# The MLP's second product with seven quarter products in place of eight

## The chip, the cores and the metric

The kernel runs on one core of a Trainium2 chip. The metric is the time of one execution on the device, in microseconds (us). TensorE (PE) multiplies matrices, VectorE (DVE), ScalarE (ACT) and GpSimd (POOL) work on elements, SyncE (SP) issues most of the loads and stores.

## The reference

One decoder block for 512 tokens of 1024 features in float32: a mixer (latent attention and a convolution branch, gated), then an MLP, each behind a norm and with a residual:

```python
m = hybrid_mixer(rms_norm(x, norm_mix_pre), ...)
x = x + rms_norm(m, norm_mix_post)
f = jnp.square(jax.nn.relu(rms_norm(x, norm_mlp_pre) @ w_ff1)) @ w_ff2   # 1024 -> 4096 -> 1024
x = x + rms_norm(f, norm_mlp_post)
```

Only the MLP's second product, `@ w_ff2`, and the steps behind it are touched.

## The kernel before

Every float32 operand of a product is split in two parts of 32 bits that PE takes in one pass each (type fp32r): ACT casts the high part, DVE (or POOL) subtracts it from the original for the low part. A product is then three matmuls (`mm3`, lines 84 to 88): high by high, high by low, low by high. A matmul takes a stationary tile of 128 x 128 and a moving tile of 128 x 512 and adds into one PSUM bank of 128 x 512. There are eight banks, under four tags: `ps` (three), `sc` (two), `cv` (two), `tp` (one).

Weights come through `wsplit` (line 99): SP loads 256 KB pieces into `raw` (six buffers), ACT casts (line 111) into `whi`, DVE subtracts (line 112) into `wlo` (four buffers each).

The first product of the MLP computes 32 tiles of 128 hidden features by 512 tokens. Tile j is eight `mm3` over the input features (`ff1_part`, line 685), into a bank `pf`; `ff1_end` (line 694) takes relu on ACT (line 696) and multiplies relu by the bank on DVE (line 699), which is the squared relu. The results stay in SBUF as 16 tiles `f1[p]` of two hidden blocks each. The first four tiles (`BRIDGE`) start on the first 256 tokens, while the last tokens' norms still run.

The second product (lines 730 to 741) holds its whole output, 4 token tiles by 2 halves of 512 columns, in the eight banks `po`. For each of the 32 hidden blocks it loads and splits one row block of w_ff2 (two pieces), splits the block of `f1` (`ff2_lhs`, line 713), and adds eight `mm3` to the banks. The last two blocks (`TAIL`) are done token tile by token tile (lines 751 to 757), so that the post-norm of one tile runs beside the products of the next: sums of squares on ACT (line 647), the inverse root on POOL (lines 649 and 145), multiplication by the gain on DVE (line 762), scale and residual on DVE (line 747), and stores by SP (line 748).

The order on each engine's queue is made when the kernel is built, by a planner: it goes through the program in written order of priority, but places an instruction when its data and a buffer are there by its own reckoning of time. A buffer of a tag is handed on when the last reader of the tile in it is done. On the chip each queue then runs in that fixed order.

The rotating buffers that matter here: `s` (six of 128 x 512, `stile`), `h` (four of 128 x 2048, of `hpool`, which hold the merged branches before), `sw` (four of 128 x 2048, which hold the MLP's input h2 in two parts), `w` (fourteen of 128 x 1024) and `ra` (four of 128 x 1024).

Of the kernel before, what the change touches and what calls it, by code (L numbers as in the profile page):

```python
# [58 lines left out]
def decoder_block(ctx: ExitStack, tc: tile.TileContext, a: dict, out: bass.AP):  # L59
# [15 lines left out]
    def stile(name, dt=F32):  # L75
        return spool.tile([P, 512], dt, tag="s", name=name, bufs=6)
# [7 lines left out]
    def mm3(o, lh, ll, rh, rl, first, last):  # L84
        """o += (lh + ll)^T (rh + rl) without the product of the two low parts (below float32's last bit)"""
        pe.matmul(o, lhsT=lh, rhs=rh, start=first, stop=False)  # L86
        pe.matmul(o, lhsT=lh, rhs=rl, start=False, stop=False)  # L87
        return pe.matmul(o, lhsT=ll, rhs=rh, start=False, stop=last)  # L88
# [10 lines left out]
    def wsplit(src, name, sizes=(512, 512), dst=None, eng=None):  # L99
        """load columns of src in pieces, split each; returns the piece (hi, lo) that holds a column range"""  # L100
        parts, off = [], 0
        for p, n in enumerate(sizes):
            raw = rtile(f"{name}_{p}", n)
            sp.dma_start(raw, src[:, off:off + n])
            if dst is None:
                hi = stage.tile([P, 512], F32R, tag="whi", name=f"whi_{name}_{p}", bufs=NSPLIT)[:, :n]
                lo = stage.tile([P, 512], F32R, tag="wlo", name=f"wlo_{name}_{p}", bufs=NSPLIT)[:, :n]
            else:
                hi, lo = (d[:, off:off + n] for d in dst)
            e = eng or pool  # L110
            recent[act] = act.copy(hi, raw)  # L111
            recent[e] = e.tensor_tensor(lo, raw, f32(hi), ALU.subtract)  # L112
            parts.append((off, n, hi, lo))
            off += n

        def cols(c0, n):
            for o, m, hi, lo in parts:
                if o <= c0 and c0 + n <= o + m:
                    return hi[:, c0 - o:c0 - o + n], lo[:, c0 - o:c0 - o + n]
            raise ValueError(f"columns {c0}:{c0 + n} of {name} lie in two pieces")  # L120

        return cols
# [53 lines left out]
    def rotary():  # L176
        """rotary tables: rows repeat every 32 partitions, sin carries the sign of its half"""
        ang = stile("ang")
# [15 lines left out]

    # the tensor engine's clock rises while it works: products that nothing reads, until the first data are there
    warm = tps("warm")
    for i in range(NWARM):
        pe.matmul(warm[:, :P], lhsT=ones, rhs=ones, start=i == 0, stop=i == NWARM - 1)

    # ---- first columns of W_in (latents, shared rope key), token rows; the pre-norm's scale of a token is  # L200
    # applied to its row of the product ----
    sp.dma_start(vecs, a["vecs"])
    xT = []
    with ExitStack() as s1:
        r1 = open_pool(s1, "r1")
        w0 = []
        for k in range(KD):
# [6 lines left out]
            w0.append(wsplit(a["w_z0"][k], f"z0{k}", (QL, Z0 - QL), (hi, lo), pool if k % 2 else dve))  # L214
        # squares of the stream, behind the splits that the first products wait for
        with ExitStack() as behind:
# [28 lines left out]
        def latents(t):  # L245
            """norms of the latents of token tile t; shared rope key, twice"""
            pa, pb = zt[t]
# [16 lines left out]
        def latents_t(t, c):  # L264
            """normalised latents to feature rows"""
            sl = slice(t * P, (t + 1) * P)
            for src, j0, n, x in ((c[0], 0, 3, "a"), (c[1], 3, 2, "b")):
                pp = cvtile(f"ct{x}{t}")
                for j in range(3):
                    pe.transpose(pp[:, j * P:(j + 1) * P], src[:, j * P:(j + 1) * P], ident)  # L270
                split_psum(cT[0][:, j0:j0 + n, sl], cT[1][:, j0:j0 + n, sl],
                           pp[:, :n * P].rearrange("p (j t) -> p j t", j=n))
            act.copy(krT[:, sl], pp[:, KL:KL + P])

        def token_scales():
            """rstd of the tokens, by partition and along the rows"""
            st_x = tps("st_x")
# [44 lines left out]

# [1 line left out]
    us = []  # L324
# [46 lines left out]
    def rope(z, name):  # L371
        """rotary embedding of two stacked heads (rows of 64), fp32"""
        sw = stile(f"sw_{name}")
# [26 lines left out]

# [1 line left out]
    att, vts, sts, qks, pms, pTs = [], {}, {}, {}, {}, {}  # L402
    with ExitStack() as s3:
        r2 = open_pool(s3, "r2")

        def project_pair(pr):
            """values (token rows) and rotary queries of a pair of heads"""
            w = wsplit(a["w_pair"][pr], f"pair{pr}", (512, QL))
# [14 lines left out]
            qr = rope(pq, f"q{pr}")  # L423
            # hi and lo of one head stacked over the rows
            st = [r2.tile([P, S], F32R, tag="qs", name=f"qs{pr}{j}", bufs=4) for j in range(2)]
# [6 lines left out]
        def project(h):  # L432
            """scaled queries and keys of a head without the rotary part, feature rows, split"""
            w = wsplit(a["w_head"][h], f"head{h}", (QL, KL))
# [78 lines left out]

# [1 line left out]
    r3 = open_pool(ctx, "r3")  # L515
# [29 lines left out]

    # causal depthwise convolution; running channel sum for the layer norm
    cs = []
# [27 lines left out]

    # layer norm over channels (partitions); sums over them through the tensor engine
    mub = cvtile("mub")
# [35 lines left out]

    # pointwise projection, gated merge
    wo = []
# [19 lines left out]

    # output projection, post-norm, residual, MLP pre-norm
    while len(wo) < KD:
# [5 lines left out]
    def square_sums(src, name, jk=None):  # L643
        """rsqrt of the mean square of two halves, plus eps"""
        ss = stat(f"ss_{name}", 2)
# [56 lines left out]
    for t in range(NT):  # L702
        prev = project_out(t, (lambda: norms(t - 1, prev)) if t else (lambda: None))
# [1 line left out]
    early = []  # L705
# [6 lines left out]

    def ff2_lhs(j):
        fh, fl = stile(f"fh{j}", F32R), stile(f"fl{j}", F32R)
        split_psum(fh, fl, f1[j // 2][:, j % 2, :])
        return fh, fl

    for j in range(NF):
        if j == NF - 2:
            first = ff2_lhs(0)  # L720
        if j < BRIDGE:
            pf, w = early[j]
            ff1_part(pf, w, SPLIT, S)
        else:
            w = wsplit(a["w_ff1"][j], f"f1{j}", eng=dve)
            pf = ps(f"pf{j}")
            ff1_part(pf, w, 0, S)
        ff1_end(j, pf)
    gout = gain("g_out", a["norm_mlp_post"], D)
    order = [tps] + [scs] * 2 + [cvtile] * 2 + [ps] * 3  # L730
    po = [[order[2 * t + hf](f"po{t}{hf}") for hf in range(2)] for t in range(NT)]
    ops = []
    for j in range(NF):
        w = wsplit(a["w_ff2"][j], f"f2{j}", eng=dve)
        fh, fl = ff2_lhs(j) if j else first
        ops.append((w, fh, fl))
        if j < NF - TAIL:
            for t in range(NT):
                sl = slice(t * P, (t + 1) * P)
                for hf in range(2):  # L740
                    mm3(po[t][hf], fh[:, sl], fl[:, sl], *w(hf * 512, 512), j == 0, False)

    def finish(t, o_, r):
        for c, n in ((0, 512), (512, 512)) if t < NT - 1 else ((0, 512), (512, 256), (768, 256)):
            hf, c1 = divmod(c, 512)
            piece = o_[:, hf, c1:c1 + n]
            dve.scalar_tensor_tensor(piece, piece, r, x1[t][hf][:, c1:c1 + n], ALU.mult, ALU.add)  # L747
            sp.dma_start(out[t * P:(t + 1) * P, c:c + n], piece)

    prev = None  # L750
    for t in range(NT):
        sl = slice(t * P, (t + 1) * P)
        o_ = wtile(f"o{t}")
        for hf in range(2):
            for j in range(NF - TAIL, NF):
                w, fh, fl = ops[j]
                mm3(po[t][hf], fh[:, sl], fl[:, sl], *w(hf * 512, 512), False, j == NF - 1)
            if hf == 0 and prev:
                finish(*prev)
        r = square_sums(po[t], f"o{t}", wtile(f"jo{t}"))  # L760
        for hf in range(2):
            dve.tensor_tensor(o_[:, hf, :], po[t][hf], gout[:, hf * 512:(hf + 1) * 512], ALU.mult)
        prev = t, o_, r
    finish(*prev)


def _layout(i):
    """Inputs as the kernel's loads take them: only reordered."""
    def rows(w):  # [K, N] -> [N/128, 128 (row in block), K/128 * 128 columns of one block]
        k, n = w.shape  # L770
        return w.reshape(k // P, P, n // P, P).transpose(2, 1, 0, 3).reshape(n // P, P, -1)
# [54 lines left out]
```

## Time and profile before

| | |
|---|---|
| time of three runs | 842.12 us median (841.9 to 844.08) |
| span of the profiled execution | 842.8 us |
| busy in that span | PE 824.0, DVE 518.8, ACT 377.0, POOL 210.1 us |
| matmuls of the second product | 768 |
| HBM read over the span | 76.76 MB |

The profile is one execution; the page gives its time as the span and lists nothing around it, so the span is its own time, and it lies inside the three runs' spread. The stretches of interest are the end of the mixer with the first tiles of the MLP (473 to 503 us), the first product (503 to 657), the second product (657 to 836), and the tail behind the last matmul (836 to 842.8). Busy times count an instruction from its start to its end, and on PE and DVE the listed times of neighbours overlap.

### The profile page before, as it was taken

Reading aid. Unit: us, or ns where it says so; the run is one execution under the profiler, and the core shown is the slowest. Engines: PE = TensorE matmul, PEld = TensorE weight load, DVE = VectorE, ACT = ScalarE, POOL = GpSimd, SP = SyncE. Lnnn points to the kernel's source line nnn. Section 1 sums busy time; section 2 is a strip of 40 time slices with the busy share of each in tenths; the row PEclk is TensorE's granted clock in tenths of the full one; section 3 lists DMA queues with packets and bytes.
Section 4 is the critical chain, followed back from the end, with each engine's and each line's share of the span. In section 5 each row is a group of like instructions: output and inputs, shape, how many; then the busy total and the mean of one; then the engine's idle time right before and its main releaser. Section 6 shows DMA issues by size and latency. Waiting matters only on the chain. (4 is left out here: it accounts for less than half of the span.)

```text
span 842.8 us, 10881 instructions
## 1 busy us (share of the span) xinstructions
PE 824.0 (98%) x3882; PEld 683.4 (81%) x3882; DVE 518.8 (62%) x838; ACT 377.0 (45%) x724; POOL 210.1 (25%) x201
## 2 busy tenths in 40 slices
PE   8989999999999999899999999999999999999996
PEld 8977888887878887687778898888888888888885
DVE  5689999999999986595554533333333333333335
ACT  7567775767572224365343333332333323332333
POOL 4244433434445446548611100000000000000001
PEclk9999999999999999899999999999999999999999
DMA  8412121222113324246440113232323232223312
GB/s 258 137 40 89 51 79 51 64 66 81 63 63 101 94 95 128 69 149 204 162 151 1 51 51 101 88 100 89 99 94 94 88 100 91 88 98 100 96 54 100
DMA packets 45126, 79.57 MB, mean 94 GB/s; under 512 B 5264, under 2 KB 10256, under 8 KB 45072
## 3 DMA queue, kind: packets, MB, share of 16 engines
q1 hardware_dynamic: 44640, 77.30, 29.0%
q0 software_dynamic: 432, 1.57, 0.5%
q8 instruction: 30, 0.49, 0.2%
q14 instruction: 24, 0.20, 0.1%
HBM read 76.76 MB, written 2.10 MB: 94 GB/s over the span
## 5 line engine op out<-in xcount | busy, mean ns | idle before, releaser
L112 DVE TENSOR_TENSOR wlo_f<-raw_f,whi_f 128x512 fp32r<-128x512 f32 x124 | 85.5, 690 | 213.3 <-ACT whi_f L111 213.1
L111 ACT CAST whi_f<-raw_f 128x512 fp32r<-128x512 f32 x124 | 76.6, 619 | 227.7 <-PE po L88 116.5
L559 DVE SCALAR_TENSOR_TENSOR cv<-u,convw,cv 128x512 f32<-128x512 f32 x232 | 161.8, 746 | 0.2
L87 PE MATMUL po<-wlo_f,fh 128*128 128x512 f32 x256 | 101.1, 395 | 0.0
L86 PE MATMUL po<-whi_f,fh 128*128 128x512 f32 x256 | 101.0, 395 | 0.0
L88 PE MATMUL po<-whi_f,fl 128*128 128x512 f32 x256 | 101.0, 395 | 0.0
L88 PE MATMUL pf<-h2h,wlo_f 128*128 128x512 f32 (+1 forms) x256 | 97.4, 381 | 0.0
L87 PE MATMUL pf<-h2l,whi_f 128*128 128x512 f32 (+1 forms) x256 | 97.4, 381 | 0.0
L86 PE MATMUL pf<-h2h,whi_f 128*128 128x512 f32 (+1 forms) x256 | 97.4, 380 | 0.0
L649 POOL TENSOR_SCALAR v_o<-ss_o 128x1 f32<-128x1 f32 x4 | 1.2, 302 | 351.5 <-ACT jo L647 351.5
L87 PEld LDWEIGHTS po<-wlo_f,fh 128*128 128x128 f32 x256 | 48.2, 188 | 11.4 <-DVE wlo_f L112 0.2
L88 PEld LDWEIGHTS po<-whi_f,fl 128*128 128x128 f32 x256 | 48.2, 188 | 11.3
L86 PEld LDWEIGHTS po<-whi_f,fh 128*128 128x128 f32 x256 | 48.2, 188 | 11.2
L112 POOL TENSOR_TENSOR wlo_gt<-raw_gt,whi_gt 128x512 fp32r<-128x512 f32 x32 | 43.9, 1374 | 50.5 <-ACT whi_gt L111 50.5
L88 PEld LDWEIGHTS pf<-h2h,wlo_f 128*128 128x128 f32 x256 | 48.2, 188 | 9.9
L87 PEld LDWEIGHTS pf<-h2l,whi_f 128*128 128x128 f32 x256 | 48.2, 188 | 9.9
L86 PEld LDWEIGHTS pf<-h2h,whi_f 128*128 128x128 f32 x256 | 48.3, 188 | 9.8
L86 PE MATMUL pg<-hTh,whi_gt 128*128 128x512 f32 x128 | 51.8, 405 | 0.0
L88 PE MATMUL pg<-hTh,wlo_gt 128*128 128x512 f32 x128 | 50.6, 395 | 0.0
L87 PE MATMUL pg<-hTl,whi_gt 128*128 128x512 f32 x128 | 50.6, 395 | 0.0
L111 ACT CAST whi_gt<-raw_gt 128x512 fp32r<-128x512 f32 x32 | 19.8, 618 | 41.3 <-PE pg L87 38.2
L86 PEld LDWEIGHTS pg<-hTh,whi_gt 128*128 128x128 f32 x128 | 24.6, 192 | 5.6 <-issue 0.5
(274 smaller groups left out, 1884.1 us busy)
## 6 DMA issues: line engine op xcount, KB each, us to landing
raw_f<-in_w_ff SPq DMA_DIRECT2D x128, 256.0 KB, 2.8
raw_gt<-in_w_zm SPq DMA_DIRECT2D x32, 256.0 KB, 2.6
raw_gb<-in_w_zm SPq DMA_DIRECT2D x16, 256.0 KB, 2.7
raw_ga<-in_w_zm SPq DMA_DIRECT2D x16, 256.0 KB, 2.6
raw_wo<-in_w_o SPq DMA_DIRECT2D x16, 256.0 KB, 2.7
raw_pw<-in_w_pw SPq DMA_DIRECT2D x16, 256.0 KB, 2.9
raw_wout<-in_w_out SPq DMA_DIRECT2D x16, 256.0 KB, 3.0
xT<-in_x_t SPq DMA_DIRECT2D x8, 256.0 KB, 4.2
```

Of the source, the lines that this page charges most:

```text
L86: pe.matmul(o, lhsT=lh, rhs=rh, start=first, stop=False)
L87: pe.matmul(o, lhsT=lh, rhs=rl, start=False, stop=False)
L88: return pe.matmul(o, lhsT=ll, rhs=rh, start=False, stop=last)
L111: recent[act] = act.copy(hi, raw)
L112: recent[e] = e.tensor_tensor(lo, raw, f32(hi), ALU.subtract)
L559: dve.scalar_tensor_tensor(co[j] if tap == CW - 1 else acc[j], src, convw[:, i, tap:tap + 1], acc[j], ALU.mult, ALU.add)
L649: pool.tensor_scalar(v, ss[:, 0:1], ss[:, 1:2], EPS, ALU.add, ALU.add)
```

## The change

The output is cut in quarters: two halves of the tokens by two halves of the columns. So are the hidden activations of a pair of blocks (two blocks by two halves of the tokens) and the four quarters of w_ff2 that belong to them (two blocks by two halves of the columns). A Strassen 2x2 scheme makes the four output quarters from seven products of quarters, for which sums and differences of quarters are formed first. Each of the seven has two banks (two token tiles of 128), and sums over the 16 pairs.

Three of the seven are computed in the loop over the first product's tiles: after each pair of tiles `first_operands` loads the pair's four quarters, forms three differences or sums of them and two of the activations, and splits them; `first_sweep` then adds the pair before to six banks (18 matmuls). While that lasts the first product's tiles have two banks left, of tag `ps`.

The other four follow behind it: `second_operands` loads the four quarters of w_ff2 again, forms one difference, splits the quarters and the activations, and `second_products` adds 24 matmuls for a pair. The three first results are copied and combined into `e`, `g` and `h` in SBUF (they free their banks). The last two pairs are done token tile by token tile, and the output quarters are put together by DVE additions (one in each token tile on POOL) before the post-norm, which now reads them from SBUF. Lines up to 712 stand as before, but for comments. The new part, cut to its core:

```diff
-    for j in range(NF):
-        ...
-    po = [[order[2 * t + hf](f"po{t}{hf}") for hf in range(2)] for t in range(NT)]
-    for j in range(NF):
-        w = wsplit(a["w_ff2"][j], f"f2{j}", eng=dve)
-        fh, fl = ff2_lhs(j) if j else first
-        ...
-                    mm3(po[t][hf], fh[:, sl], fl[:, sl], *w(hf * 512, 512), j == 0, False)
+    half = (slice(0, 2 * P), slice(2 * P, S))
+    NP = NF // 2
+    def quarter(j, hf, tag="raw", bufs=NRAW):
+        raw = stage.tile([P, 512], F32, tag=tag, name=f"f2{j}{hf}", bufs=bufs)
+        sp.dma_start(raw, a["w_ff2"][j][:, hf * 512:(hf + 1) * 512])
+        return raw
+    def split(hi, lo, src):
+        act.copy(hi, src)
+        dve.tensor_tensor(lo, src, f32(hi), ALU.subtract)
+    def products(bank, left, right, first, last, toks=(0, 1)):
+        for t in toks:
+            sl = slice(t * P, (t + 1) * P)
+            mm3(bank[t], left[0][:, sl], left[1][:, sl], *right, first, last)
+    def first_operands(p):
+        f = f1[p]
+        b12, b22, b11, b21 = (quarter(2 * p + r, c) for r, c in ((0, 1), (1, 1), (0, 0), (1, 0)))
+        w = [htile(f"x{x}{p}") for x in "hl"]
+        s23 = stile(f"s23{p}")
+        a22 = stile(f"a22{p}", F32R)
+        split(a22[:, half[0]], a22[:, half[1]], f[:, 1, half[1]])
+        dve.tensor_tensor(s23[:, half[1]], f[:, 0, half[0]], f[:, 0, half[1]], ALU.subtract)
+        dve.tensor_tensor(f[:, 0, half[1]], f[:, 0, half[1]], f[:, 1, half[1]], ALU.add)
+        dve.tensor_tensor(s23[:, half[0]], f[:, 0, half[1]], f[:, 0, half[0]], ALU.subtract)
+        split(w[0][:, 3, :], w[1][:, 3, :], s23)
+        ts = [stile(f"t{n}{p}") for n in (3, 2, 4)]
+        for n, (t, x, y, op) in enumerate(((ts[0], b22, b12, ALU.subtract), (ts[1], ts[0], b11, ALU.add), (ts[2], ts[1], b21, ALU.subtract))):
+            dve.tensor_tensor(t, x, y, op)
+            split(w[0][:, n, :], w[1][:, n, :], t)
+        dve.tensor_tensor(f[:, 1, half[1]], f[:, 1, half[0]], s23[:, half[0]], ALU.subtract)
+        s2, s3 = ([x[:, 3, h] for x in w] for h in half)
+        return (s3, s2, [a22[:, h] for h in half]), w
+    def second_operands(p):
+        b12, b11, b21, b22 = (quarter(2 * p + r, c, *t) for r, c, *t in (
+            (0, 1, "whi", NSPLIT), (0, 0), (1, 0), (1, 1)))
+        t1 = stage.tile([P, 512], F32, tag="wlo", name=f"t1{p}", bufs=NSPLIT)
+        l = htile(f"l{p}")
+        w = [r3.tile([P, 4, 512], F32R, tag="sw", name=f"y{x}{p}", bufs=4) for x in "hl"]
+        split(l[:, 0:2, :], l[:, 2:4, :], f1[p])
+        split(w[0][:, 0, :], w[1][:, 0, :], b11)
+        dve.tensor_tensor(t1, b12, b11, ALU.subtract)
+        for n, src in ((1, t1), (2, b21), (3, b22)):
+            split(w[0][:, n, :], w[1][:, n, :], src)
+        return l, w
+    ops = {}
+    for p in range(NP):
+        for j in (2 * p, 2 * p + 1):
+            ...
+            ff1_end(j, pf)
+        ops[p] = first_operands(p)
+        if p == 1:
+            acc = [[scs(f"p70"), scs("p71")], [cvtile("p60"), cvtile("p61")], [tps("p40"), ps("p41")]]
+        if p:
+            first_sweep(p - 1, ops.pop(p - 1))
+    second = second_operands(0)
+    bcc = [[ps(f"p1{t}") for t in range(2)]]
+    second_products(0, second, (0,))
+    first_sweep(NP - 1, ops.pop(NP - 1))
+    ...
+    for t in range(2):
+        act.copy(e[:, t, :], acc[1][t])
+        dve.tensor_tensor(g[:, t, :], acc[0][t], e[:, t, :], ALU.add)
+        dve.tensor_tensor(h[:, t, :], g[:, t, :], acc[2][t], ALU.subtract)
+    bcc += [[cvtile(f"p5{t}") for t in range(2)], [scs(f"p2{t}") for t in range(2)], [tps("p30"), ps("p31")]]
+    second_products(0, second, (1, 2, 3))
+    for p in range(1, NP - TAIL):
+        second_products(p, second_operands(p), range(4))
+    def post(t):
+        src = [o_[t][:, hf, :] for hf in range(2)]
+        r = square_sums(src, f"o{t}")
+        for hf in range(2):
+            dve.tensor_tensor(src[hf], src[hf], gout[:, hf * 512:(hf + 1) * 512], ALU.mult)
+        finish(t, r)
+    last = [(p, second_operands(p)) for p in range(NP - TAIL, NP)]
+    for t in range(2):
+        v = stile(f"v{t}")
+        for n in (0, 1, 2, 3):
+            for p, x in last:
+                second_products(p, x, (n,), (t,))
+            bank = bcc[n][t]
+            if n == 0:
+                act.copy(v, bank)
+                dve.tensor_tensor(o_[t + 2][:, 0, :], v, h[:, t, :], ALU.add)
+            elif n == 1:
+                dve.tensor_tensor(g[:, t, :], g[:, t, :], bank, ALU.add)
+                dve.tensor_tensor(e[:, t, :], e[:, t, :], bank, ALU.add)
+                dve.tensor_tensor(o_[t + 2][:, 1, :], g[:, t, :], v, ALU.add)
+                post(t + 2)
+                pool.tensor_tensor(e[:, t, :], e[:, t, :], v, ALU.add)
+            elif n == 2:
+                dve.tensor_tensor(o_[t][:, 0, :], v, bank, ALU.add)
+            else:
+                dve.tensor_tensor(o_[t][:, 1, :], e[:, t, :], bank, ALU.add)
+                post(t)
```

`htile` gives a buffer of tag `h`; `first_sweep` calls `products` for the three banks of `acc`, `second_products` for the chosen ones of the four in `bcc`; `finish` is scale, residual and store as before.

## Rows read from the trace of the kernel before

**Rows 1.** The page, busy time of each engine (share of the span, instructions).
```profile
PE 824.0 (98%) x3882; PEld 683.4 (81%) x3882; DVE 518.8 (62%) x838; ACT 377.0 (45%) x724; POOL 210.1 (25%) x201
```
**Rows 2.** Busy time by stretch (start:end, length, engines, clock, DMA share, GB/s).
```profile
core 0: us, PE busy (x) PEld busy (x) DVE busy (x) ACT busy (x) POOL busy (x), PEclk, DMA share, GB/s
385.00:400.00 15.00, 14.31 (x62) 11.23 (x61) 7.79 (x9) 6.93 (x13) 12.25 (x10) 1.00 0.69 226
...
503.00:657.00 154.00, 154.00 (x664) 124.83 (x664) 54.86 (x83) 48.11 (x83) 0.00 (x0) 1.00 0.29 93
657.00:825.00 168.00, 168.00 (x725) 136.19 (x724) 57.86 (x92) 51.37 (x93) 0.00 (x0) 1.00 0.28 88
...
836.00:843.00 7.00, 0.00 (x0) 0.00 (x0) 3.00 (x6) 0.57 (x2) 0.86 (x2) 0.73 0.42 151
```
**Rows 3.** Instructions on tile po: ns min/median/max, first and last start in us.
```profile
L86 PE MATMUL po<-whi_f,fh x256: 390/393/404, 657.1 to 835.0; 128*128 128x512 f32 x128
```
**Rows 4.** Groups by line and shape, 470 to 843: busy us, mean ns, idle before.
```profile
L112 DVE TENSOR_TENSOR wlo_f<-raw_f,whi_f 128x512 fp32r<-128x512 f32 x120 | 82.8, 690 | 213.3 <-ACT whi_f L111 213.1
L111 ACT CAST whi_f<-raw_f 128x512 fp32r<-128x512 f32 x120 | 74.3, 619 | 227.7 <-PE po L88 116.5 <-PE pf L87 111.2
...
L699 DVE TENSOR_TENSOR f<-pf,rl 128x512 f32<-128x512 f32 x32 | 21.9, 684 | 3.9 <-ACT rl L696 3.9
...
L696 ACT ACTIVATE rl<-pf 128x512 f32<-128x512 f32 x32 | 19.0, 595 | 4.2 <-PE pf L88 4.2
```
**Rows 5.** Timeline of DVE where its queue is full: start us, length us, instruction.
```profile
363.72 1.27 DVE L606 TENSOR_TENSOR c<-c,rsb 128x512 f32<-128x512 f32 x2
364.92 0.68 DVE L612 TENSOR_TENSOR swl<-si,swh 128x512 fp32r<-128x512 f32 x1
...
366.57 1.19 DVE L610 TENSOR_TENSOR si<-si,c 128x512 f32<-128x512 f32 x1
```
**Rows 6.** Loads by tile, 385 to 400 and then 657 to 825: count, KB, landing us.
```profile
raw_wout<-in_w_out SPq DMA_DIRECT2D x5, 256.0 KB, 3.8
...
raw_f<-in_w_ff SPq DMA_DIRECT2D x55, 256.0 KB, 2.9
```
**Rows 7.** Timeline of ACT in the first product; idle before in brackets, with its end's cause.
```profile
640.35 0.62 ACT L111 CAST whi_f<-raw_f 128x512 fp32r<-128x512 f32 x1 [2.16 <-PE pf L87]
640.88 0.59 ACT L696 ACTIVATE rl<-pf 128x512 f32<-128x512 f32 x1
```
**Rows 8.** Instructions on tile ah of 1024 columns: ns min/median/max, starts.
```profile
L534 ACT CAST ah<-att x4: 1032/1054/1063, 244.4 to 250.0; 128x1024 fp32r<-128x1024 f32 x4
L535 DVE TENSOR_TENSOR al<-att,ah x4: 1211/1296/2289, 245.5 to 252.7; 128x1024 fp32r<-128x1024 f32 x4
```
**Rows 9.** Timeline of the tail.
```profile
834.85 1.41 DVE L747 SCALAR_TENSOR_TENSOR o<-o,r_o,x 128x512 f32<-128x512 f32 x2 [0.16 <-POOL r_o L145]
...
835.45 0.40 PE L88 MATMUL po<-whi_f,fl 128*128 128x512 f32 x1
...
835.88 0.60 ACT L647 ACTIVATE jo<-po 128x512 f32<-128x512 f32 x1 [0.65 <-PE po L88]
836.18 1.28 DVE L762 TENSOR_TENSOR o<-po,g_out 128x512 f32<-128x512 f32 x2
...
836.67 0.30 POOL L649 TENSOR_SCALAR v_o<-ss_o 128x1 f32<-128x1 f32 x1 [1.85 <-ACT jo L647]
837.05 0.56 POOL L145 TENSOR_TENSOR r_o<-v_o,mhalf 128x1 f32<-128x1 f32 x1
837.64 1.54 DVE L747 SCALAR_TENSOR_TENSOR o<-o,r_o,x 128x512 f32<-128x512 f32 x3 [0.18 <-POOL r_o L145]
```
**Rows 10.** Timeline of POOL beside rows 5.
```profile
365.83 1.38 POOL L112 TENSOR_TENSOR wlo_gt<-raw_gt,whi_gt 128x512 fp32r<-128x512 f32 x1 [2.58 <-ACT whi_gt L111]
```

More of the change, by code (lines that the diff above doesn't have):

```diff
@@ L711, in decoder_block @@
         early.append((pf, w))
[L713 to L716, printed above, removed]
-    for j in range(NF):
[L719 to L728, printed above, removed]
@@ L729, in decoder_block @@
-    gout = gain("g_out", a["norm_mlp_post"], D)
-    order = [tps] + [scs] * 2 + [cvtile] * 2 + [ps] * 3
-    po = [[order[2 * t + hf](f"po{t}{hf}") for hf in range(2)] for t in range(NT)]
-    ops = []
-    for j in range(NF):
-        w = wsplit(a["w_ff2"][j], f"f2{j}", eng=dve)
-        fh, fl = ff2_lhs(j) if j else first
[L736 to L740, printed above, removed]
-                    mm3(po[t][hf], fh[:, sl], fl[:, sl], *w(hf * 512, 512), j == 0, False)
@@ L743, in finish @@
-    def finish(t, o_, r):
-        for c, n in ((0, 512), (512, 512)) if t < NT - 1 else ((0, 512), (512, 256), (768, 256)):
+    half = (slice(0, 2 * P), slice(2 * P, S))
[7 more added lines that the diff above has]
+        dve.tensor_tensor(lo, src, f32(hi), ALU.subtract)
@@ new lines, in products, with htile @@
+    def products(bank, left, right, first, last, toks=(0, 1)):
+        for t in toks:
+            sl = slice(t * P, (t + 1) * P)
+            mm3(bank[t], left[0][:, sl], left[1][:, sl], *right, first, last)
+    def htile(name, dt=F32R):
+        return hpool.tile([P, 4, S], dt, tag="h", name=name, bufs=4)
+    def first_operands(p):
[16 more added lines that the diff above has]
+        return (s3, s2, [a22[:, h] for h in half]), w
@@ new lines, in first_sweep @@
+    def first_sweep(p, ops):
+        left, w = ops
+        for n, (bank, l) in enumerate(zip(acc, left)):
+            products(bank, l, [x[:, n, :] for x in w], p == 0, p == NP - 1)
+    def second_operands(p):
[10 more added lines that the diff above has]
+        return l, w
@@ new lines, in decoder_block, with second_products @@
+    LEFT = ((0, 0), (0, 1), (1, 0), (1, 1))
+    def second_products(p, ops, which, toks=(0, 1)):
+        l, w = ops
+        for n in which:
+            r, c = LEFT[n]
+            products(bcc[n], [l[:, r, half[c]], l[:, 2 + r, half[c]]], [x[:, n, :] for x in w], p == 0, p == NP - 1, toks)
+    ops = {}
+    for p in range(NP):
+        for j in (2 * p, 2 * p + 1):
+            if j < BRIDGE:
+                pf, w = early[j]
+                ff1_part(pf, w, SPLIT, S)
+            else:
+                w = wsplit(a["w_ff1"][j], f"f1{j}", eng=dve)
+                pf = ps(f"pf{j}")
+                ff1_part(pf, w, 0, S)
+            ff1_end(j, pf)
[4 more added lines that the diff above has]
+            first_sweep(p - 1, ops.pop(p - 1))
@@ new lines, in decoder_block @@
+    gout = gain("g_out", a["norm_mlp_post"], D)
+    second = second_operands(0)
+    bcc = [[ps(f"p1{t}") for t in range(2)]]
+    second_products(0, second, (0,))
+    first_sweep(NP - 1, ops.pop(NP - 1))
+    e, g = (ratile(n) for n in ("e", "g"))
+    h = wtile("h")
+    for t in range(2):
[3 more added lines that the diff above has]
+    bcc += [[cvtile(f"p5{t}") for t in range(2)], [scs(f"p2{t}") for t in range(2)], [tps("p30"), ps("p31")]]
@@ L745, in finish @@
+    second_products(0, second, (1, 2, 3))
+    for p in range(1, NP - TAIL):
+        second_products(p, second_operands(p), range(4))
+    o_ = [wtile(f"o{t}") for t in range(NT)]
+    def finish(t, r):
+        for c, n in ((0, 512), (512, 512)) if t != 1 else ((0, 512), (512, 256), (768, 256)):
             hf, c1 = divmod(c, 512)
-            piece = o_[:, hf, c1:c1 + n]
+            piece = o_[t][:, hf, c1:c1 + n]
             dve.scalar_tensor_tensor(piece, piece, r, x1[t][hf][:, c1:c1 + n], ALU.mult, ALU.add)
@@ L748, in finish @@
             sp.dma_start(out[t * P:(t + 1) * P, c:c + n], piece)
[L750 to L753, printed above, removed]
+    def post(t):
+        src = [o_[t][:, hf, :] for hf in range(2)]
+        r = square_sums(src, f"o{t}")
         for hf in range(2):
[L755 to L763, printed above, removed]
@@ L764, in decoder_block @@
-    finish(*prev)
+            dve.tensor_tensor(src[hf], src[hf], gout[:, hf * 512:(hf + 1) * 512], ALU.mult)
[18 more added lines that the diff above has]
+                dve.tensor_tensor(o_[t][:, 0, :], v, bank, ALU.add)
+            else:
+                dve.tensor_tensor(o_[t][:, 1, :], e[:, t, :], bank, ALU.add)
+                post(t)
```

## The prediction

> **What bounds the kernel now.** I read the page's busy times first: TensorE (PE) is busy for 824.0 of 842.8 us, VectorE (DVE) for 62% and ScalarE (ACT) for 45% [rows 1]. Then I cut the MLP into stages [rows 2]. In the first product (503 to 657) and the second (657 to 825) PE is busy in every microsecond at full granted clock, while DVE works 36% and 34% of the time, ACT about 31%, and the loads run at 93 and 88 GB/s. Here only fewer matmuls can save time, and there is room beside PE. Behind 836 PE is done and DVE works 3 of 7 us: this tail belongs to DVE, ACT, POOL and the stores.
>
> A matmul's listed time isn't its price. The second product's 256 matmuls of line 86 start between 657.1 and 835.0, and lines 87 and 88 put two more behind each [rows 3]: 177.9 / (255 x 3) = 0.2326 us from start to start. The listed 0.393 us overlaps with the next one.
>
> **Matmuls removed.** Before: 32 blocks x 4 token tiles x 2 halves x 3 = 768. After: 16 pairs of blocks x 7 quarter products x 2 token tiles x 3 = 672, of the same shape (128 x 128 against 128 x 512). 96 x 0.2326 = **22.3 us less**. Whether this arrives depends on what the sums and differences of the scheme cost, stage by stage.
>
> **First stage: three products between the first product's tiles.** A pair of tiles now takes PE 48 + 18 = 66 matmuls, 15.35 us. Beside it:
> - DVE per pair: 4 low parts of w_ff1, 2 squares, 3 differences of quarters, 4 low parts of differences: 13 of 512 columns; and 5 of 256. A 512-column one takes 0.69 us [rows 4], but in a full queue the next starts 0.60 us later (two in 1.27, the next at 364.92) [rows 5]. 256 columns cost between half of that and all of it; I take 0.40. 13 x 0.60 + 5 x 0.40 = 9.8 us, 64% of 15.35.
> - ACT: 8 casts at 0.62, 2 at 0.59, one of 256 columns: under 6.8 us, 44%.
> - Loads: 8 of 256 KB in place of 4, 2.1 MB in 15.35 us, 137 GB/s. The trace has 226 GB/s over 15 us [rows 2], with a median landing of up to 3.8 us against 2.9 in the second product [rows 6].
>
> The chain that hangs on the pair's second tile is relu 0.60, square 0.68 [rows 4], about four narrow steps (1.6), cast 0.62, low part 0.69, with hand-overs about 4.3 us. Its reader, the sweep, comes a whole pair later, behind two tiles (11.2 us). The differences of w_ff2 wait only for loads and for the buffers of two sweeps ago, free before the pair's tiles start. That holds if the queues aren't in written order, and they aren't: the cast for a coming tile (its buffer just freed by the tile that ends) stands ahead of the ended tile's relu, two tiles ahead of its written place [rows 7]. One PSUM bank less for the tiles of the first product (two, not three) costs nothing: relu and square need 1.3 us of 5.6 us. So 0; bounds 0 to 3 us, if one difference in each of 15 pairs comes 0.2 us late.
>
> **Entry into the second stage.** The four buffers of the second operands are h2's, free when the last tile's products end; the activations' split (l) takes buffers that the sweep of pair 14 frees 4.2 us later. From there a cast of 1024 columns (1.05) and a low part (1.21 to 1.30) [rows 8] go before quarter product 1 can start: 2.3 us. Sweep 15 (4.2 us) is ready to run in that gap. But g and h (4 DVE steps on PSUM), the first two l and ten steps for the first two sets of quarters all fall into the next 8 us: 2.4 + 2.4 + 6.0 = 10.8 us of DVE, some of it early. I take 1 us; bounds 0 (sweep 15 covers all) and 4 (it covers nothing, plus the backlog).
>
> **Second stage, steady.** A pair has 24 matmuls, 5.58 us. DVE needs 1.21 + 5 x 0.60 = 4.2 us (75%), or 4.8 at listed times; ACT 1.05 + 4 x 0.62 = 3.5 us; loads 1.05 MB, 188 GB/s, below the 226 seen. The quarters have two sets of buffers, so set p+2 starts when pair p is done: first quarter after about 1.5 us, fourth after 3.7, needed at 5.58. PE stays the bound: 0, bounds 0 and 10 us (0.7 us a pair, case C).
>
> **Last two pairs.** Set 15 can start only when pair 13 ends, and pair 14's first three matmuls (0.7 us) run out before its low part is there (1.5 us). I take 0.6; bounds 0 and 3 (PE waits for all four quarters).
>
> **The tail is the larger price.** Call Q the end of pair 13. PE has 48 matmuls left, 11.2 us, and ends at Q + 11.8. In that stretch DVE gets, for each of two token tiles, 6 additions, 4 multiplications by the gain and 4 steps of scale and residual (5 in the second, two of them of 256 columns): 20 at 0.60, 7 at 0.66 (two in 1.41) and 2 at 0.40 [rows 5, 9] = 17.4 us, more than PE's 11.2. The first can start at Q + 2.8 (the bank's six matmuls and a copy of 0.6). So the last ends at Q + 20.2 at the earliest. POOL adds twice over 128 x 512: while it did such work (365.83 to 367.21), a DVE multiplication with both inputs in SBUF took 1.19 us in place of 0.68 [rows 5, 10]. One such delay each, 0.5 to 0.6, makes Q + 21.3: 9.5 us behind PE. Now the last DVE step ends at 837.64 + 1.54 = 839.18, 3.3 us behind the last matmul (835.85) [rows 9]. So **6.2 us more**, the stores behind it unchanged. Bounds: 0.8 (only the new last addition, 0.69 and a hand-over) and 8.5 (every step at its listed time).
>
> The Trainium skill speaks against the cheap queue used here: "VectorE: DVE Perf Modes", section "The DRAIN you can't avoid", says that the next DVE instruction doesn't issue until the pipeline is empty. Rows 5 disagree for independent steps. By the rule the tail would be 2.3 us longer (20 x 0.68 + 7 x 0.75 + 2 x 0.48 = 19.8), the time 830.0. On the POOL additions, "SBUF — State Buffer", section "Who interferes with whom", has an exclusive lock for just this pair of instructions; the 1.19 us agrees in direction.
>
> **Sum.** -22.3 + 0 + 1 + 0 + 0.6 + 6.2 = -14.5 us against the profiled execution's 842.8. Its span stands 0.7 us above the median of the runs (842.12, spread 841.9 to 844.08), so I forecast 842.1 - 14.5 = **827.6 us**.
>
> **Rivals.**
> - A, the forecast: 824 to 831.
> - B, the tail overlaps better: steps of the first token tile are through before the second needs DVE, and only the new addition shows, with no stall. -22.3 + 0.8 = 820.6. For it: DVE is two thirds idle now. Against: 17.4 us of steps in 11.2 us of products.
> - C, the hand-over paces the second stage. With DVE at listed times (4.8 us) plus waits for each cast (rows 4 show DVE's idle time ending on just these casts), a pair takes 6.1 to 6.3 us, not 5.58: 14 x 0.6 = 8 us more, about 835. For it: 75% load and strict buffers. Against: each quarter has 1.9 us or more of slack.
> - D, the other side: first-stage stalls in every pair. Place: DVE's queue behind the pair's second tile. If the weights' low part of the next tile stands behind the pair's chain, PE has only the sweep, 4.2 us, to cover 4.3 + 0.62 + 0.69 = 5.6 us and hand-overs: 1.7 us a pair, 14 x 1.7 = 24 us, 827.6 + 24 = 852, and more if the differences of w_ff2 stand there too. It decides once that chain exceeds 4.2 us. Against: the order of rows 7, and weights two tiles ahead.
> - E, C and a long entry together give it all back: about 841. That the scheme doesn't remove the matmuls is excluded by the count.
>
> **Numbers.** A 0.50, B 0.12, C 0.21, D 0.10, E 0.07. Under 0.3% (2.5 us) a measurement of this kernel can't tell from no change. Faster: A, B and nearly all of C, 0.82; same: E and the edge of C, 0.08; slower: D, 0.10. The range 820 to 838 holds A, B and most of C.
>
> **What would show it.** Right: 672 matmuls of the second product 0.2326 us apart; PE busy throughout both stages; DVE near 64% in the first and 75% in the second; last DVE step 9 to 10 us behind the last matmul, DVE without gaps there. Wrong: regular PE gaps per pair that end on a DVE low part (C in the second stage, D in the first), or SP's loads late with PE waiting on a cast. If PE's pitch changes, the first term falls.

## The result and the profile after

| | before | after |
|---|---|---|
| median of four runs each | 843.10 us (841.9 to 844.18) | 831.35 us (829.35 to 833.51) |
| ratio after / before | | 0.986 (95%: 0.9835 to 0.9884) |
| span of the profiled execution | 842.8 us | 828.4 us |
| matmuls of the second product | 768 | 672 |
| HBM read | 76.76 MB | 93.54 MB |

The change gains 11.75 us, 1.4%. The forecast was 827.6 us, a gain of 14.5. The time lies inside the stated range (820 to 838), 3.75 us above the point and 0.35 above the forecast's own band (A, 824 to 831).

Medians and spans don't measure the same stretch: the profiled execution of the changed kernel has a time of 830.19 us and a span of 828.4, and in the runs of all the changed kernels on record the time is the span plus 1.7 to 1.9. So the span of before, 842.8, stands for a time of about 844.6 (an estimate from this difference), and not for its own time, as the section on the time before has it. The forecast isn't touched by that, since it starts from the median.

The page after, busy time of each engine (share of the span, instructions); it answers [rows 1]:

```profile
PE 797.4 (96%) x3786; PEld 660.7 (80%) x3786; DVE 633.0 (76%) x1046; ACT 419.7 (51%) x792; POOL 215.6 (26%) x203
```

PE lost 27 us of listed busy time, and DVE, which had 519, now works 633 us. Where the two meet is seen by stretch, in the view of [rows 2]:

```profile
core 0: us, PE busy (x) PEld busy (x) DVE busy (x) ACT busy (x) POOL busy (x), PEclk, DMA share, GB/s
600.00:650.00 50.00, 50.00 (x218) 40.67 (x217) 31.50 (x57) 19.55 (x35) 0.00 (x0) 1.00 0.39 133
700.00:720.00 20.00, 18.02 (x79) 14.35 (x78) 14.13 (x27) 9.68 (x18) 0.00 (x0) 1.00 0.60 198
720.00:740.00 20.00, 20.00 (x87) 16.14 (x86) 19.23 (x28) 12.47 (x20) 0.00 (x0) 1.00 0.50 168
760.00:780.00 20.00, 20.00 (x87) 16.08 (x87) 15.00 (x22) 11.17 (x19) 0.00 (x0) 1.00 0.52 177
812.00:828.40 16.40, 0.10 (x1) 0.00 (x0) 11.67 (x18) 3.15 (x9) 5.28 (x7) 0.63 0.27 97
```

In the first stage (600 to 650) PE is busy throughout with DVE at 63%; in the second (760 to 780) again, with DVE at 75%. At the start of the second (720 to 740) DVE is at 96%, the entry's sums among its steps, and PE doesn't wait there either. Two stretches fall short: 700 to 720, where PE misses 2.0 us, and the last, 16.3 us in which PE has nothing left and DVE works 18 instructions.

**One clock for both kernels.** The spans differ by 14.4 us, nearly the forecast, but 3.2 us of that lie ahead of the change. The first matmul of the MLP starts at 477.1 before and at 474.0 after:

```profile
L86 PE MATMUL pf<-h2h,whi_f x256: 279/392/404, 477.1 to 656.4; 128*128 128x512 f32 x112, 128*128 128x256 f32 x16
```

```profile
L86 PE MATMUL pf<-h2h,whi_f x256: 279/392/404, 474.0 to 711.1; 128*128 128x512 f32 x112, 128*128 128x256 f32 x16
```

Up to there PE's instructions stand in the same order in both, and in all eight kernels of the experiments too. In these ten traces the first matmul of the MLP starts anywhere between 473.95 and 478.24 us, in three of the changed kernels later than before. So the 3.2 us don't belong to the change. One thing that differs is the mean granted clock (the column ahead of the last two), here for two stretches of before and then the same two of after:

```profile
50.00:100.00 50.00, 46.22 (x231) 37.73 (x230) 45.63 (x77) 37.44 (x71) 21.86 (x26) 0.97 0.18 57
...
300.00:350.00 50.00, 47.03 (x198) 38.02 (x197) 36.18 (x54) 17.20 (x29) 29.93 (x23) 0.94 0.34 105
```

```profile
50.00:100.00 50.00, 45.78 (x235) 37.37 (x234) 46.64 (x81) 37.99 (x74) 22.20 (x26) 1.00 0.19 60
...
300.00:350.00 50.00, 47.03 (x201) 37.82 (x200) 34.96 (x53) 17.41 (x29) 29.30 (x24) 0.97 0.30 100
```

The clock of before is lower by 0.03 in both. Instruction by instruction, PE before falls 1.0 us behind PE after between 46 and 61 us and 1.2 us between 345 and 361, in or next to these stretches; the remaining 1.0 us arises elsewhere, most of it where the column says 1.00 in both, and its cause is not shown. From here on everything is measured from the first matmul of the MLP, where this spread is out. Such a table can be read off each trace (one profiled execution each):

| us | first matmul to end of the last | PE's gap in it | last matmul to the last DVE step | to the end of the span | all from the first matmul |
|---|---|---|---|---|---|
| before | 358.70 | 0 | 3.34 | 6.94 | 365.65 |
| after | 338.14 | 1.98 | 13.12 | 16.32 | 354.46 |
| e1_pool | 337.22 | 1.10 | 13.63 | 16.82 | 354.04 |
| e2_banks | 336.61 | 0.84 | 3.40 | 6.59 | 343.20 |
| e3_double | 358.03 | 0 | 13.15 | 16.33 | 374.36 |
| e4_loads | 337.42 | 1.29 | 13.11 | 16.77 | 354.20 |
| e5_early | 336.84 | 0.38 | 13.10 | 16.29 | 353.13 |
| e6_dve2 | 337.70 | 1.58 | 16.21 | 19.39 | 357.10 |
| e8_tail4 | 337.55 | 1.42 | 7.18 | 10.37 | 347.92 |
| e9_best | 336.33 | 0.05 | 5.85 | 9.03 | 345.36 |

By it the change gives 365.65 - 354.46 = 11.19 us, near the 11.75 of the medians: PE's stretch 20.56 less, the tail 9.38 more. The last matmul after, and then the timeline of DVE in the tail after (start us, length us, instruction, idle before in brackets); it answers [rows 9]:

```profile
811.70 0.40 PE L88 MATMUL p<-yh,l 128*128 128x512 f32 x1
```

```profile
803.71 0.69 DVE L843 TENSOR_TENSOR o<-v,h 128x512 f32<-128x512 f32 x1
804.31 0.68 DVE L845 TENSOR_TENSOR g<-g,p 128x512 f32<-128x512 f32 x1
804.90 0.68 DVE L846 TENSOR_TENSOR e<-e,p 128x512 f32<-128x512 f32 x1
805.50 0.69 DVE L847 TENSOR_TENSOR o<-g,v 128x512 f32<-128x512 f32 x1
806.11 1.79 DVE L831 TENSOR_TENSOR o<-o,g_out 128x512 f32<-128x512 f32 x1
...
811.54 0.68 DVE L845 TENSOR_TENSOR g<-g,p 128x512 f32<-128x512 f32 x1
...
813.28 1.42 DVE L824 SCALAR_TENSOR_TENSOR o<-o,r_o,x 128x512 f32<-128x512 f32 x2 [0.45 <-POOL r_o L145]
814.61 0.68 DVE L843 TENSOR_TENSOR o<-v,h 128x512 f32<-128x512 f32 x1
...
816.41 1.75 DVE L831 TENSOR_TENSOR o<-o,g_out 128x512 f32<-128x512 f32 x1
...
822.14 0.69 DVE L831 TENSOR_TENSOR o<-o,g_out 128x512 f32<-128x512 f32 x1 [0.25 <-ACT j_o L647]
823.67 1.54 DVE L824 SCALAR_TENSOR_TENSOR o<-o,r_o,x 128x512 f32<-128x512 f32 x3 [0.85 <-POOL r_o L145]
```

PE ends at 812.1. There DVE has only begun with the second token tile's sums (811.54; the next is at 814.61), and its last step ends at 825.2. In 21.5 us from 803.71 it is idle for 1.55. So the tail can be read as a difference: the steps from the first sum on take 21.5 us, the first sum starts 8.4 us ahead of PE's end, and 13.1 us stick out behind it.

### The profile page after: what moved, and what is told of

It is laid out like the page before. It is cut to its first block, busy times and chain, and to the rows that moved or that the text cites. A ratio compares the mean times of both kernels' runs of the same rounds, so it can differ in the third digit from the quotient of the medians.

```text
span 828.4 us, 11002 instructions
## 1 busy us (share of the span) xinstructions
PE 797.4 (96%) x3786; PEld 660.7 (80%) x3786; DVE 633.0 (76%) x1046; ACT 419.7 (51%) x792; POOL 215.6 (26%) x203
## 3 DMA queue, kind: packets, MB, share of 16 engines
HBM read 93.54 MB, written 2.10 MB: 115 GB/s over the span
## 5 line engine op out<-in xcount | busy, mean ns | idle before, releaser
L112 DVE TENSOR_TENSOR wlo_f<-raw_f,whi_f 128x512 fp32r<-128x512 f32 x60 | 41.1, 690 | 65.1 <-ACT whi_f L111 63.9
L849 POOL TENSOR_TENSOR e<-e,v 128x512 f32<-128x512 f32 x2 | 3.2, 1600 | 329.4 <-DVE e L846 329.4
L111 ACT CAST whi_f<-raw_f 128x512 fp32r<-128x512 f32 x60 | 36.9, 621 | 85.0 <-PE pf L87 50.0
L86 PE MATMUL p<-yh,l 128*128 128x512 f32 x128 | 50.4, 395 | 0.0
L87 PE MATMUL p<-yl,l 128*128 128x512 f32 x128 | 50.4, 395 | 0.0
L88 PE MATMUL p<-yh,l 128*128 128x512 f32 x128 | 50.2, 395 | 0.0
L726 ACT CAST yh<-f 128x512 fp32r<-128x512 f32 x48 | 28.0, 617 | 36.8 <-PE p L87 27.6
L727 DVE TENSOR_TENSOR yl<-f,yh 128x512 fp32r<-128x512 f32 x48 | 31.7, 687 | 14.8 <-ACT yh L726 14.7
L726 ACT CAST xh<-t 128x512 fp32r<-128x512 f32 x48 | 29.6, 619 | 19.5 <-DVE t L751 19.5
L727 DVE TENSOR_TENSOR xl<-t,xh 128x512 fp32r<-128x512 f32 x48 | 31.5, 684 | 0.5 <-ACT xh L726 0.5
```

Source lines behind the costliest of these rows:

```text
L726: act.copy(hi, src)
L727: dve.tensor_tensor(lo, src, f32(hi), ALU.subtract)
L849: pool.tensor_tensor(e[:, t, :], e[:, t, :], v, ALU.add)
```

## Experiments

The theory after the result: PE gave back the matmuls' whole time, and DVE's queue behind the last pairs took 9.4 us of it. Rivals: the second stage loses time to loads or hand-overs; or matmuls are worth less than their pitch.

**e3_double: the price of 96 matmuls.**

```diff
+        products(acc[1], left[1], [x[:, 1, :] for x in w], False, p == NP - 1)
```

> One of the three products of the first stage is added twice: 96 matmuls more of the same shape, no other work. Theory (TensorE sets the time in both stages, 0.2326 us a matmul): 22.3 us more, some 853.7, and the distance of the last VectorE step from the last matmul stays 13 us. Rival (TensorE has slack between the tiles of the first product, which would mean that taking out matmuls gives less than their time): under 15 us more.

Measured: 852.67 us median, 21.3 above the changed kernel; PE's stretch without its gap 358.03 - 336.16 = 21.87 longer, tail 16.33. PE sets the time between the first product's tiles too: the rival's 15 us or less is out. The one gap is not there in this kernel, whose sweeps are six matmuls (1.4 us) longer; that their length filled it was not tried apart. Before to after gives 358.70 - 336.16 = 22.54 for the same 96.

**e2_banks: the tail without the sums.**

```diff
-            if n == 0:
-                act.copy(v, bank)
-                ...
+            if n % 2 == 1:
+                post((t + 2, t)[n // 2], [bcc[n - 1][t], bank])
```

> Leaves out the additions that put the output quarters together behind the last products: norm, gain and residual read four of the banks directly. Theory (the tail grew because VectorE has more steps than the last products cover): VectorE then has 5.1 us of steps a token tile under 5.6 us of products, the last step ends 3.5 to 5 us behind the last matmul as in the kernel before, and the time falls by 8 to 9.5 us to some 822. Rival (what is missing of the matmuls' 22 us is lost in the second stage, to loads or hand-overs): under 3 us less.

Measured: 822.83 us, 8.5 us less than the changed kernel in the medians and 11.3 from the first matmul; tail 6.59, last DVE step 3.40 behind the last matmul. The tail's growth is the sums' and what hangs on them (the copies, GpSimd's additions, multiplications that read SBUF in place of a bank), and none of it was lost in the second stage. Timeline of DVE in this kernel's tail:

```profile
812.04 1.28 DVE L830 TENSOR_TENSOR o<-p,g_out 128x512 f32<-128x512 f32 x2
813.51 1.41 DVE L824 SCALAR_TENSOR_TENSOR o<-o,r_o,x 128x512 f32<-128x512 f32 x2 [0.18 <-POOL r_o L145]
814.84 1.28 DVE L830 TENSOR_TENSOR o<-p,g_out 128x512 f32<-128x512 f32 x2
816.36 1.54 DVE L824 SCALAR_TENSOR_TENSOR o<-o,r_o,x 128x512 f32<-128x512 f32 x3 [0.24 <-POOL r_o L145]
```

**e1_pool: GpSimd's two additions gone.**

```diff
-                dve.tensor_tensor(g[:, t, :], g[:, t, :], bank, ALU.add)
-                dve.tensor_tensor(e[:, t, :], e[:, t, :], bank, ALU.add)
-                dve.tensor_tensor(o_[t + 2][:, 1, :], g[:, t, :], v, ALU.add)
+                u = stile(f"u{t}")
+                dve.tensor_tensor(u, v, bank, ALU.add)
+                dve.tensor_tensor(o_[t + 2][:, 1, :], g[:, t, :], u, ALU.add)
                 post(t + 2)
-                pool.tensor_tensor(e[:, t, :], e[:, t, :], v, ALU.add)
+                dve.tensor_tensor(e[:, t, :], e[:, t, :], u, ALU.add)
```

> The sums v + P5 are formed once on VectorE and added to g and to e, so that GpSimd has no addition in the tail; VectorE has as many steps as before. Theory (the tail is VectorE's queue, and each GpSimd addition holds one of its steps for 1.1 us): no VectorE step of 1.7 us is left in the tail, the last one ends about 11 us behind the last matmul in place of 13.1, and the time falls by about 2 us to some 829. Rival (the GpSimd additions run beside VectorE for nothing): no change, within 1 us.

Measured: 831.65 us, no change; the tail 16.82 in place of 16.32. The number is the rival's, but its reason is not: the long steps went with the additions, so these do hold VectorE. Only the gain did not come. Timeline of DVE, this kernel, from the first token tile's second multiplication:

```profile
808.33 0.68 DVE L831 TENSOR_TENSOR o<-o,g_out 128x512 f32<-128x512 f32 x1
809.78 1.42 DVE L824 SCALAR_TENSOR_TENSOR o<-o,r_o,x 128x512 f32<-128x512 f32 x2 [0.76 <-POOL r_o L145]
...
812.58 0.69 DVE L831 TENSOR_TENSOR o<-o,g_out 128x512 f32<-128x512 f32 x1 [0.19 <-ACT j_o L647]
814.12 1.42 DVE L824 SCALAR_TENSOR_TENSOR o<-o,r_o,x 128x512 f32<-128x512 f32 x2 [0.84 <-POOL r_o L145]
...
818.45 0.69 DVE L849 TENSOR_TENSOR e<-e,u 128x512 f32<-128x512 f32 x1
819.05 0.69 DVE L831 TENSOR_TENSOR o<-o,g_out 128x512 f32<-128x512 f32 x1
820.58 1.41 DVE L824 SCALAR_TENSOR_TENSOR o<-o,r_o,x 128x512 f32<-128x512 f32 x2 [0.84 <-POOL r_o L145]
...
823.44 0.69 DVE L831 TENSOR_TENSOR o<-o,g_out 128x512 f32<-128x512 f32 x1 [0.25 <-ACT j_o L647]
824.97 1.54 DVE L824 SCALAR_TENSOR_TENSOR o<-o,r_o,x 128x512 f32<-128x512 f32 x3 [0.84 <-POOL r_o L145]
```

Idle time rose from 1.55 to 3.72 us: in the fixed order DVE now comes to each scaling before the inverse root is there, and waits for POOL. The 2.2 us turned into another wait. My expectation failed because it counted DVE's steps alone and not the chain of squares and inverse root that runs beside them. Part of that chain also became longer: GpSimd's step at line 649 took 0.62 us for token tile 2 and again for tile 3 in the changed kernel, and takes 1.03 and 1.12 us here.

**e4_loads: a quarter of the loads.**

```diff
-        b12, b11, b21, b22 = (quarter(2 * p + r, c, *t) for r, c, *t in (...))
+        b12 = quarter(2 * p, 1, "whi", NSPLIT)
+        b11 = b21 = b22 = b12
```

> Leaves out three of the four loads of a pair in the second stage: the one quarter that is still loaded is split in place of the other three, so that all other work stays. Theory (the second stage is TensorE's, its loads of 188 GB/s are covered): TensorE's stretch from the first tile of the MLP to the last matmul, 338.1 us, shrinks by no more than the one gap of 2.0 us at the entry, where a cast also waited 1.7 us for a landing. Rival (loads slow matmuls or hand-overs in the second stage): 3 us less or more.

Measured: 832.65 us; PE's stretch 337.42 against 338.14, the gap 1.29 against 1.98. The loads of the second stage cost PE nothing beyond, at most, part of that gap, which varies as much between kernels with all loads.

**e6_dve2: DVE filled in the second stage.**

```diff
             split(w[0][:, n, :], w[1][:, n, :], src)
+            if n < 3:
+                dve.tensor_tensor(w[1][:, n, :], src, f32(w[0][:, n, :]), ALU.subtract)
```

> Two of the four low parts of the second stage are written twice: VectorE has 5.4 us of steps a pair in place of 4.2, under 5.58 us of matmuls. Theory (buffers for two pairs cover the hand-over, so VectorE may be filled nearly to TensorE's time): TensorE's stretch grows by under 2 us. Rival (the hand-over of buffers needs VectorE's free time): 0.6 us or more a pair, 8 us or more in all.

Measured: 836.48 us, 5.1 us more in the median, and 357.10 against 354.46 from the first matmul, 2.6. (Of the 6.9 us between the two spans, 4.3 lie ahead of the MLP.) PE's stretch is unchanged (337.70). Busy time by stretch of this kernel, and DVE in its tail:

```profile
760.00:780.00 20.00, 20.00 (x87) 16.12 (x86) 20.00 (x30) 12.58 (x20) 0.00 (x0) 1.00 0.58 191
780.00:800.00 20.00, 20.00 (x87) 16.08 (x86) 19.86 (x30) 10.45 (x18) 0.00 (x0) 1.00 0.57 180
```

```profile
809.42 0.68 DVE L845 TENSOR_TENSOR o<-v,h 128x512 f32<-128x512 f32 x1
811.33 0.69 DVE L853 TENSOR_TENSOR o<-v,p 128x512 f32<-128x512 f32 x1 [1.22 <-PE p L88]
```

DVE is full and PE doesn't miss a microsecond: the buffers do cover the hand-over, as expected of PE's stretch. But DVE comes late out of the stage, and the tail grows by 3.07 to 19.39, which I had not expected. The first sum starts 6.5 us ahead of PE's end in place of 8.4: 1.9 us. The other 1.2 is a wait for PE at 811.33, where this kernel's queue has the sums in another order than the changed kernel's (line 853 ahead of 847); so that part isn't the queue's length.

**e5_early: the gap ahead of the last sweep.** In the changed kernel PE waited once:

```profile
715.65 0.40 PE L88 MATMUL p<-xh,a 128*128 128x512 f32 x1
718.03 0.73 PE L86 MATMUL p<-xh 128*128 128x512 f32 x2 [1.98 <-ACT xh L726]
```

ACT's queue there (start, length, idle before in brackets): a cast for the second stage waits 1.72 us for its load, and behind it stand two casts of differences, and only then the activations' cast (s) that PE needs.

```profile
715.80 0.62 ACT L726 CAST yh<-f 128x512 fp32r<-128x512 f32 x1 [1.72 <-DMA f<-in_w_ff]
716.33 1.13 ACT L726 CAST xh<-t 128x512 fp32r<-128x512 f32 x2
717.37 0.61 ACT L726 CAST xh<-s 128x512 fp32r<-128x512 f32 x1
```

```diff
+            if j % 2 == 0:
+                x = differences(p)
-        ops[p] = first_operands(p)
+        ops[p] = first_operands(p, x)
```

> The differences of the quarters of w_ff2 stand in the program between the two tiles of a pair, ahead of the steps that wait for the second tile. Theory (TensorE's one gap, 2.0 us ahead of the last sweep, comes of the last pair's differences and casts standing in the queues ahead of the activation's cast): the gap goes, the time falls by 1.5 to 2 us, to some 829.5. Rival (the gap is the landing of the loads, which stay as they are): the gap stays near 2 us and so does the time.

Measured: 830.56 us; the gap 0.38, and 353.13 against 354.46 from the first matmul, 1.3 us less, under the 1.5 to 2 expected. The medians alone (0.8 us) don't tell it from none. The gap is 0.84 to 1.98 in the kernels that leave this order as it was and have the same sweep, and 0.38 and 0.05 in the two that move the differences. So the order most likely makes most of it, as far as one trace of each kernel can say; its size varies, and e4 (1.29) doesn't settle how much of the rest is loads.

**e8_tail4: more products over the sums.**

```diff
-TAIL = 2
+TAIL = 4
+        else:
+            w = [[wtile(f"y{x}{p}{q}", F32R) for x in "hl"] for q in range(2)]
```

> The last four pairs, not two, are done token tile by token tile; the second operands of the last two have buffers of their own for that (of the tag w, whose activations are used up by then). Theory (VectorE's 8.7 us of steps for a token tile lie under 5.6 us of products, and would be covered under 11.2): the last VectorE step ends 4 to 6 us behind the last matmul in place of 13.1, the whole tail is 7.5 to 9.5 us in place of 16.3, and the time falls by 7 to 9 us, to some 823. Rival (the tail is the chain of squares, inverse root, scaling and store of the last token tile, whatever came before): under 3 us less.

Measured: 826.08 us, ratio to before 0.9789 (0.9758 to 0.982). The time is 5.3 us below the changed kernel's, where 7 to 9 were expected, and beyond the rival's 3. The tail is 10.37, 5.95 less; 7.5 to 9.5 was expected, and the last DVE step, expected 4 to 6 us behind the last matmul, is 7.18 behind it. DVE in its tail, and one of GpSimd's additions:

```profile
799.00 0.69 DVE L848 TENSOR_TENSOR o<-v,h 128x512 f32<-128x512 f32 x1
...
814.41 1.41 DVE L829 SCALAR_TENSOR_TENSOR o<-o,r_o,x 128x512 f32<-128x512 f32 x2 [0.85 <-POOL r_o L145]
...
818.81 1.54 DVE L829 SCALAR_TENSOR_TENSOR o<-o,r_o,x 128x512 f32<-128x512 f32 x3 [0.85 <-POOL r_o L145]
```

```profile
810.79 2.22 POOL L854 TENSOR_TENSOR e<-e,v 128x512 f32<-128x512 f32 x1 [3.45 <-DVE e L851]
```

From the first sum on DVE's steps take 21.4 us, as in the changed kernel (21.5), but the first sum now starts 14.2 us ahead of PE's end (813.17) in place of 8.4. Cover is what was missing. The expected 4 to 6 us would have needed a shorter stretch too, and DVE still waits twice for the inverse root, the first time behind GpSimd's addition, which ends at 813.01.

**e9_best: the three together.**

> The four-pair tail, the early differences of the weights and the sums v + P5 on VectorE together. Theory: the gap at the last sweep (1.6 us of 2.0) and the tail (about 8 us) both go, and with VectorE covered the two GpSimd additions don't matter: some 821 us. Rival (the gains overlap, since an earlier end of the matmuls only lengthens the tail): no better than the four-pair tail alone.

Measured: 823.87 us, ratio to before 0.9765 (0.9741 to 0.979), the lowest median of the kernels that compute the whole output but above the 821 expected: 7.5 us below the changed kernel, 9.1 from the first matmul. No gap over 0.05 us, tail 9.03. Against e8_tail4 it is 2.2 us less in the medians, with spreads that overlap (822.71 to 826.66 against 825.31 to 826.73), and 2.56 from the first matmul: 1.22 in PE's stretch and 1.34 in the tail. So the rival (no better than four pairs alone) is unlikely but not out, and the expectation that GpSimd's additions no longer matter fits badly with the shorter tail. DVE in its tail:

```profile
812.62 0.68 DVE L860 TENSOR_TENSOR o<-v,p 128x512 f32<-128x512 f32 x1
813.22 0.68 DVE L862 TENSOR_TENSOR o<-e,p 128x512 f32<-128x512 f32 x1
...
816.33 1.54 DVE L833 SCALAR_TENSOR_TENSOR o<-o,r_o,x 128x512 f32<-128x512 f32 x3 [0.84 <-POOL r_o L145]
```

PE ends at 812.0 here, just before the last two sums of the output.

## Why the prediction was right, and where it was off

- **Matmuls removed**, -22.3: measured -22.5 (PE's stretch without the gap), and 21.9 in e3 for the same number added. Right.
- **First stage**, 0: PE 50.00 of 50.00 us, DVE 63% (forecast 64%), loads 133 GB/s (137). Case D did not happen.
- **Entry**, +1, bounds 0 to 4: 1.98 us, for another reason than the one worked out, so that it was luck that the size came near. No wait of PE ends on the split of l. The step that failed is that sweep 15 is "ready to run": in the queues the last pair's differences stand between the steps of its chain, and one cast waits for a load. In the pairs before, the next two tiles cover this; the last pair has none behind it.
- **Second stage**, 0: PE 20.00 of 20.00 us and no wait in it. Case C did not happen, and e6 shows that even a full DVE doesn't bring it about; it shows the price elsewhere.
- **Last two pairs**, +0.6: no gap was found there. The forecast counted these 0.6 us as cover for the tail too, so most of what was gained here was missing there.
- **Tail**, +6.2, bounds 0.8 and 8.5: measured +9.38, above its own upper bound. This is the mis-sized term, the mechanism being the one forecast. The last DVE step is 13.12 us behind the last matmul, not 9.5, and the stretch behind that step is 0.4 us shorter than before (3.20 against 3.60). Of the 3.6 us, 0.6 is the first sum's lead (8.4 us ahead of PE's end, not 9.0: PE ended 11.4 us behind pair 13, not 11.8, and the sum started 3.0 behind it, not 2.8), 1.1 the two multiplications beside GpSimd's additions, which took 1.79 and 1.75 us (1.1 more each, where I took half of that from [rows 5, 10]), and 1.55 the waits on ACT and POOL, for which I had nothing: "DVE without gaps there" did not hold. Some 0.35 is left over. e1 shows that the long multiplications and the waits aren't independent: without the first the second grow.

The terms sum to -22.5 + 2.0 + 9.4 = -11.1 us, against -14.5. The tail's cheap DVE queue held: steps of 0.69 follow each other at 0.60 us (804.31, 804.90, 805.50 in the same queue). The section of the Trainium skill that the prediction sets against this ("VectorE: DVE Perf Modes", "The DRAIN you can't avoid") goes on to say that an instruction that isn't held starts earlier; so the section doesn't speak against this queue, and the 0.60 us agree with its exception.

## What to carry to other kernels

In this kernel arithmetic taken off the bounding engine arrived in full where the others had room all along, and was in part lost at the end, where the work that replaces it had nothing left to hide under. So count the cheap engine's steps against the products that are still to come behind them, and schedule the last blocks so that the products outlast them (here four pairs in place of two, 5.3 us). In a queue of fixed order, removing a stall helps only as far as what stands next in the queue is ready earlier too (e1). And a queue may be full without slowing its neighbour, and still be late for what follows (e6).

## What was not expected of the hardware

The lines are GpSimd's in the tail after, then one in e1_pool:

```profile
805.73 1.62 POOL L849 TENSOR_TENSOR e<-e,v 128x512 f32<-128x512 f32 x1 [326.58 <-DVE e L846]
...
811.88 0.30 POOL L649 TENSOR_SCALAR v_o<-ss_o 128x1 f32<-128x1 f32 x1 [3.17 <-ACT j_o L647]
```

```profile
818.78 1.12 POOL L649 TENSOR_SCALAR v_o<-ss_o 128x1 f32<-128x1 f32 x1 [4.70 <-ACT j_o L647]
```

While GpSimd added 128 x 512 in 1.62 us, the VectorE multiplication that started 0.4 us later, with both inputs in SBUF, took 1.79 us in place of 0.68 and ended 0.55 us behind the addition.

The delay goes the other way too, and in these traces it goes with what VectorE reads, not with how full its queue is. GpSimd's one-column step took 1.12 us beside two VectorE steps with both inputs in SBUF (818.45 and 819.05 in e1_pool) and ended 0.2 us behind the second. It took 0.30 us in the middle of a full VectorE queue, beside a step that reads a bank (811.54 in the tail after), and 0.30 all four times in e2_banks, where VectorE's multiplications read banks, as before [rows 9].
